# Layer 0 of a hybrid decoder trunk: a written-out TensorE order for the S5 quarters, the projections, the gates and the linear unit

## The chip, the cores and the metric

The kernel runs on one core of a Trainium2 chip. The metric is the device time of one execution in microseconds (us). The engines are named as the profile names them: PE (TensorE, matrix products; PEld its weight loads), DVE (VectorE), ACT (ScalarE), POOL (GpSimd) and SP (SyncE, which here issues every DMA).

## The reference

The reference takes `x` of 1024 tokens by 1024 features through two residual layers, all in float32. The change touches layer 0 alone:

```python
def even_layer(hn, ...):
    q, k, v, gate_a, u, gate_b = split_cols(hn @ w_in, EVEN_SPLITS)   # 512, 128, 128, 512, 512, 512
    q = rms_norm(q.reshape(bsz, L, 8, 64), q_g)
    k = rms_norm(k.reshape(bsz, L, 2, 64), k_g)
    att = swa_sink_attention(q, k, v, sinks, rel_bias) * jax.nn.silu(gate_a)
    ssm = s5_mixer(u, ...) * jax.nn.silu(gate_b)
    return jnp.concatenate([att, ssm], axis=-1) @ w_out
```

`swa_sink_attention` is banded: each block of 128 queries sees its own and the previous block of keys, with a bias by distance and a sink in the softmax. `s5_mixer` is a complex diagonal state space (32 groups of 16 channels, 64 states), then `gelu`, then the gated linear unit `h = y @ glu_w + glu_b`, `h[:, :512] * sigmoid(h[:, 512:])`. Layer 1 (an indexer that picks the top 256 keys, attention over them, gate, output projection) stays as it is.

## The kernel before, in words

Activations lie transposed, features on the partitions. Each float32 product is made of three fp32r products: both factors are split into a high part and the rest, and hi x hi, hi x lo, lo x hi are summed in PSUM. Weights come as a stream of chunks of 256 output columns (`wstream`; `load_w`, L135): one DMA of 1 MB, a copy to `whi` on ACT (L153) and a subtraction to `wlo` on POOL or DVE (L154). Chunks listed in `LO_ON_V` (L126) are split in four pieces with DVE; the others in one piece of 128x2048 with POOL.

Layer 0 has these stages in the order of the program text:

- The first chunk of `u` is projected while `x` arrives (L317 to L341); the squares give the RMS factors `rr` and, by a round trip through DRAM, `rb` (L342 to L349).
- S5 parameters on DVE (L393 to L516), from scalars to the powers of the decay.
- `u_chunk(0)`, then keys and values (L541 to L556): eight token tiles of 24 products of 256 columns, per-head norms in `norm_heads` (L351: squares on ACT with a sum each, `rstd_of` L197 and a product with `rr` on POOL at L199, L200 and L360, scaled copies on ACT at L362), a transposition by PE.
- The distance table `gt` (32 copies, L563 to L567, on DVE).
- Four S5 quarters (`s5_quarter`, L578). Each builds `Q` (DVE, L602 to L607), `W` (POOL, L609 to L616) and the rotations `Tb` (DVE, L623 to L628), transposes `Q` (L635), makes a small kernel matrix `M` (L640 to L654, with eight DMAs), multiplies the states' input (L663, 32 products), scans on DVE (L667 to L687: products with `Tb`, eight scans, the result `X`), and gets the output by L694 (with `M`) and L696 (with `X`), with a gelu on ACT (L698). `u_chunk(1)` stands after the first quarter.
- `q_chunk(0)` and `q_chunk(1)` (L367): 16 tiles of 24 products of 256 columns with the same norms, two transpositions each (L375), then out to DRAM.
- The banded attention: 16 units (8 blocks by 2 key heads). `swa_scores` (L743) makes eight score products, adds the bias and takes the maximum on DVE (L756), exponentials on ACT (L761) and the division on DVE or POOL. `swa_out` (L771) runs `SWA_AHEAD` = 4 units later: transpositions (L777), copies, products with `v` (L783).
- `gate_chunk` four times (L382): 16 groups of 48 products of 256 columns, a product with `rb` on DVE (L389), out to DRAM unactivated.
- The linear unit (L810 to L868): `y` is split into `y_hi` and `y_lo` (L822, L823), eight groups of 24 products of 512 columns (L855 to L857), Sigmoid of the linear unit's gate (L861) and of the branch's gate (L863), three products and the split into `cat` (L864 to L868). Then the attention's result is read back, gated by Sigmoid (L875), two products, and split into `cat` (L876 to L879).
- The output projection and the residual (L886 to L919), then layer 1.

Only SP's queue has a written order at the very start (L310). On all other engines a list scheduler orders the instructions of layer 0 at build time, by the program's order as priority and by its own estimate of durations; each engine then runs its list strictly in order. So PE runs the gates, which stand after the attention in the text, among the S5 quarters and the attention. Layer 1 has two stretches with a written PE order (`manual_schedule`, L1083 and L1555); there a `Filler` (L1385) draws pieces of other work between the steps of the main work.

## Time and profile before

| what | value |
|---|---|
| median of three runs | 1107.06 us (1104.15 to 1111.34) |
| profiled execution, its own time | 1109.46 us |
| its span on the core | 1107.7 us |
| mean granted PE clock | 0.971 |
| PE, DVE, ACT, POOL busy | 93%, 72%, 54%, 43% of the span |

Between the profiled execution's time and its span lie 1.8 us. Times in rows count from the start of the span. Busy is the time in which at least one instruction of the engine runs; "idle before" is the gap ahead of an instruction, with what ended it. Matrix products overlap, so the distance from the start of one to the start of the next is what one costs in a row of them. PEclk is the mean share of full clock granted in a stretch; the granted level is either 1.0 (2.4 GHz) or 0.5 (1.2 GHz). The stretch in which the change lies runs from 43 us (end of the first `u` chunk) to 418 us (first product of the output projection).

### The profile page before, as it was taken

The numbers are of one execution on the slowest core, as the hardware profiler recorded it, in microseconds if no ns is written. First come the engines' busy times: TensorE is split into PE (matmuls) and PEld (weight loads), VectorE is DVE, ScalarE is ACT, GpSimd is POOL, SyncE is SP. The second block draws the span as 40 slices with busy tenths as digits, with TensorE's granted clock in tenths as the row PEclk, the third lists the DMA queues.
The fourth block names the chain that finished last, engine by engine and source line by source line (L and its number), as shares of the span: only waits on it lengthen the run. The fifth ranks groups of instructions, "written<-read, shape, count | busy, mean of one in ns | idle before, by whom it ended". The sixth has DMA issues, their size and how long they took to land.

```text
span 1107.7 us, 19105 instructions
## 1 busy us (share of the span) xinstructions
PE 1026.0 (93%) x6533; PEld 900.1 (81%) x6533; DVE 797.0 (72%) x1768; ACT 598.6 (54%) x1563; POOL 475.7 (43%) x667
## 2 busy tenths in 40 slices
PE   6799888999999789999799999999998889999998
PEld 4687877898776567887689999999886768998898
DVE  6899987717553795367668759889877989778742
ACT  7343554215543642344356699969954777565620
POOL 3356876232121283224322367867522554445000
PEclk9899998999999889999899999999999999999999
DMA  7228542683321623545002103022326686665323
GB/s 257 96 78 272 147 123 65 173 235 127 95 77 39 247 80 110 199 166 164 4 1 96 63 29 102 39 87 78 115 77 201 213 263 176 190 196 163 113 91 119
DMA packets 105585, 143.05 MB, mean 129 GB/s; under 512 B 9568, under 2 KB 80104, under 8 KB 100624
## 3 DMA queue, kind: packets, MB, share of 16 engines
q1 hardware_dynamic: 105488, 141.84, 40.9%
q8 instruction: 51, 0.84, 0.3%
q14 instruction: 46, 0.38, 0.1%
HBM read 104.93 MB, written 38.31 MB: 129 GB/s over the span
## 4 chain that ended last, share of the span: by engine, by line
PE 60%; DVE 19%; DMA 7%; ACT 5%; issue 4%; POOL 4%; SPq 1%; DVEq 0%; ACTq 0%; POOLq 0%
PE mm L230 7%; PE mm L231 7%; PE mm L232 7%; PE mm L217 4%; PE mm L216 4%; PE mm L218 4%; PE psx L783 2%; PE mm L1497 2%; PE mm L1498 2%; PE mm L1496 2%; PE tr L1365 2%; DMA xt<-in_xT_dram 1%; DVE xh L917 1%; PE tr L777 1%; PE mm L1380 1%
## 5 line engine op out<-in xcount | busy, mean ns | idle before, releaser
L154 POOL TENSOR_TENSOR wlo<-wraw,whi 128x512 fp32r<-128x512 f32 (+1 forms) x43 | 95.0, 2233 | 120.5 <-ACT whi L153 107.6
L153 ACT CAST whi<-wraw 128x512 fp32r<-128x512 f32 (+2 forms) x117 | 83.5, 770 | 79.6 <-PE mm L231 29.2
L1338 POOL TENSOR_TENSOR bt<-bt,mk 128x384 f32<-128x384 f32 (+3 forms) x80 | 85.4, 1084 | 77.7 <-DMA bt<-g_d 70.2
L216 PE MATMUL mm<-whi,h1T_hi 128*128 128x256 f32 x384 | 110.5, 289 | 0.0
L218 PE MATMUL mm<-whi,h1T_lo 128*128 128x256 f32 x384 | 110.0, 288 | 0.0
L217 PE MATMUL mm<-wlo,h1T_hi 128*128 128x256 f32 x384 | 109.9, 287 | 0.0
L1199 DVE TENSOR_SCALAR_CACHE_REDUCE vjunk<-sc,vt 128x512 bf16<-128x512 uint16 (+5 forms) x90 | 91.1, 1012 | 3.0
L230 PE MATMUL mm<-hT_hi,whi 128*128 128x256 f32 (+1 forms) x288 | 87.5, 304 | 0.6 <-DVE uT L533 0.6
L231 PE MATMUL mm<-hT_lo,whi 128*128 128x256 f32 (+1 forms) x288 | 87.1, 302 | 0.0
L232 PE MATMUL mm<-hT_hi,wlo 128*128 128x256 f32 (+1 forms) x288 | 86.9, 302 | 0.0
L1233 ACT ACTIVATE sjunk<-sc,st 128x384 bf16<-128x384 uint16 (+5 forms) x90 | 77.2, 858 | 6.4 <-POOL st L1237 4.1
L154 DVE TENSOR_TENSOR wlo<-wraw,whi 128x512 fp32r<-128x512 f32 (+1 forms) x74 | 57.6, 815 | 24.9 <-ACT whi L153 20.6
L1496 PE MATMUL mm<-aT_hi,whi 128*128 128x256 f32 x256 | 73.5, 287 | 1.2 <-ACT aT_hi L1470 1.2
L1497 PE MATMUL mm<-aT_lo,whi 128*128 128x256 f32 x256 | 73.1, 285 | 1.0 <-DVE aT_lo L1471 1.0
L216 PEld LDWEIGHTS mm<-whi,h1T_hi 128*128 128x128 f32 x384 | 73.1, 191 | 0.6
L217 PEld LDWEIGHTS mm<-wlo,h1T_hi 128*128 128x128 f32 x384 | 73.2, 191 | 0.3
L218 PEld LDWEIGHTS mm<-whi,h1T_lo 128*128 128x128 f32 x384 | 73.1, 191 | 0.3
L1498 PE MATMUL mm<-aT_hi,wlo 128*128 128x256 f32 x256 | 73.2, 286 | 0.0
L362 ACT ACTIVATE st<-mm,nr 128x64 f32<-128x64 f32 (+1 forms) x160 | 45.4, 356 | 51.0 <-POOL nr L360 47.0
L1056 DVE SCALAR_TENSOR_TENSOR sc<-relu,wi,sc 128x384 f32<-128x384 f32 (+3 forms) x70 | 49.4, 707 | 20.5 <-ACT relu L1051 16.6
L1349 ACT ACTIVATE s<-s,mn 128x128 f32<-128x128 f32 (+7 forms) x64 | 49.5, 774 | 26.6 <-DVE mn L1343 26.5
L216 PE MATMUL mm<-whi,hT_hi 128*128 128x256 f32 x192 | 58.0, 303 | 4.4 <-ACT st L362 2.7
(386 smaller groups left out, 3515.9 us busy)
## 6 DMA issues: line engine op xcount, KB each, us to landing
wraw<-in_w_dram SPq DMA_DIRECT2D x20, 1024.0 KB, 5.2
wraw<-in_wo_dram SPq DMA_DIRECT2D x16, 1024.0 KB, 5.4
bt<-g_d SPq DMA_DIRECT2D x24, 256.0 KB, 3.7
g_d<-g1r_d SPq DMA_DIRECT2D x8, 576.0 KB, 9.1
bt<-g_d SPq DMA_DIRECT2D x24, 192.0 KB, 3.2
qT_d<-gst SPq DMA_DIRECT2D x32, 128.0 KB, 2.1
qT<-qT_d SPq DMA_DIRECT2D x32, 128.0 KB, 3.1
xh<-in_xT_dram SPq DMA_DIRECT2D x16, 256.0 KB, 3.2
```

Source lines behind the costliest of these rows:

```text
L154: eng.tensor_sub(lo[p_], raw[p_], rd(hi[p_]))
L216: T.matmul(ps, a, hi[:, k, c0:c1], start=(k == 0), stop=False)
L217: T.matmul(ps, a, lo[:, k, c0:c1], start=False, stop=False)
L218: T.matmul(ps, b, hi[:, k, c0:c1], start=False, stop=(k == 7))
L230: T.matmul(o, a, hT[0][:, k, ts], start=(k == 0), stop=False)
L231: T.matmul(o, a, hT[1][:, k, ts], start=False, stop=False)
L232: T.matmul(o, b, hT[0][:, k, ts], start=False, stop=(k == 7))
L1199: V.tensor_scalar(junk[:, :128 * (b + 1)], data(b), self.thr(j), None, op0=OP.is_ge, op1=OP.add, accum_out=self.cnt[:, it, j:j + 1])
L1338: G.tensor_add(bt, bt, mk[b][:, ks])
L1496: T.matmul(ps, a, aT[0][:, k, toks], start=(k == 0), stop=False)
L1497: T.matmul(ps, a, aT[1][:, k, toks], start=False, stop=False)
L1498: T.matmul(ps, b, aT[0][:, k, toks], start=False, stop=(k == 7))
```

## The change

The list of what it does:

- From the keys and values on to the end of the linear unit, PE's order is the order of the text (`manual_schedule` for PE). All other engines keep the list scheduler.
- Projections, gates and the linear unit become one generator of pieces (`fill`): keys and values, `u_chunk(1)`, the two `q` chunks, the four gate chunks, the linear unit. A piece carries an estimate in us. `fill(us)` draws pieces for so much estimated time. Transpositions behind the norms are drawn `LAG` = 7.0 estimated us after the products of their tile.
- `s5_quarter` is cut at six places. `fill` is called ahead of the quarters (36), after each of four parts of a quarter (4, 4, 16, 6) and once ahead of the attention (12); `Q` and `Tb` of the next quarter are emitted two parts ahead.
- The attention is cut finer: a unit's four score pairs alternate with transpositions of an earlier unit and with products with `v` of the one before that; `fill(1.1)` stands twice in each unit until four of the eight groups of the linear unit are done. The other four groups follow the attention.
- A gate group has 24 products of 512 columns in place of 48 of 256; at its eviction the silu is made by `x * (1 + tanh(x/2))` (twice the silu) with one ACT and one more DVE operation; halves and quarters are put right later. The gate of the attention is applied as the attention leaves PSUM, that of the S5 branch in the linear unit's eviction, whose result goes to DRAM (`go_d`) and comes back for the split into `cat`.
- `rstd_of` and the product with `rr` are emitted at high priority for keys and queries; `gt` is filled by ACT; every weight chunk is split in four pieces; `s` has 4 buffers in place of 6, `nms` 4 in place of 2.

```diff
+LAG = 7.0
+S5_FILL = (36.0, 4.0, 4.0, 16.0, 6.0, 12.0)
+SWA_FILL = 1.1
...
-        return (hi, lo), [piece, WSTEP if i in LO_ON_V or i == 21 else 8, 0]
+        return (hi, lo), [piece, WSTEP, 0]
...
-        r = rstd_of(stg, ms[:, :nh], nh, "nr")
-        if t is not None:
-            G.tensor_tensor(r, r, bc(rr[:, 0, t:t + 1], [128, nh]), op=OP.mult)
+        with tc.high_priority() if t is not None else ExitStack():
+            r = rstd_of(stg, ms[:, :nh], nh, "nr")
+            if t is not None:
+                G.tensor_tensor(r, r, bc(rr[:, 0, t:t + 1], [128, nh]), op=OP.mult)
...
+    def lagged(n, products, rest):
+        for i in range(n):
+            out = products(i)
+            later.append([LAG, lambda i=i, out=out: rest(i, out)])
+            yield 2.8
...
+    def gate0_pieces(dst, f0):
+        w = wstream.get()
+        for f in range(2):
+            for half in range(2):
+                ps = ps_mm.tile([128, 512], F32, name="mm")
+                for k in range(8):
+                    a, b_ = (x[:, k, f * 128:f * 128 + 128] for x in w)
+                    h_, l_ = (x[:, k, half * 512:half * 512 + 512] for x in hT)
+                    T.matmul(ps, a, h_, start=(k == 0), stop=False)
+                    T.matmul(ps, a, l_, start=False, stop=False)
+                    T.matmul(ps, b_, h_, start=False, stop=(k == 7))
+                    if k % 2 and k < 7:
+                        yield 1.4
                 st = stg.tile([128, 512], F32, name="gst", bufs=2)
                 V.tensor_mul(st, ps, rb[:, half * 512:(half + 1) * 512])
+                S.activation(ps, st, AF.Tanh, scale=0.5)
+                V.scalar_tensor_tensor(st, ps, 1.0, st, op0=OP.add, op1=OP.mult)
                 dma(dst[f0 + f, :, half * 512:(half + 1) * 512], st)
+                yield 1.4
...
+    class Filler:
+        def __call__(self, us):
+            self.owed += us
+            while self.owed > 0:
+                got = next(self.gen, None)
+                if got is None:
+                    break
+                self.owed -= got
+                for x in later:
+                    x[0] -= got
+                while later and later[0][0] <= 0:
+                    later.pop(0)[1]()
...
+    def glu_pieces():
+        es_h0.close()
...
+                S.copy(yh, yv)
+                V.tensor_sub(yl, yv, rd(yh))
+        yield 0.0
...
+                    S.activation(sg, pp[0], AF.Tanh, scale=0.5, bias=glub[:, 1, 4 + n:5 + n])
+                    V.scalar_tensor_tensor(sg, sg, 1.0, gt_, op0=OP.add, op1=OP.mult)
+                    V.scalar_tensor_tensor(sg, pp[1], glub[:, 0, n:n + 1], sg, op0=OP.add, op1=OP.mult)
+                    dma(go_d[n, :, t0:t0 + 512], sg)
+                    glu_done.append(n)
+                    yield 1.4
...
+    fill = Filler(chain(kv_pieces(), u_pieces(1), q_pieces(0), q_pieces(1), gate0_pieces(ga_d, 0), gate0_pieces(ga_d, 2),
+                        gate0_pieces(gb_d, 0), gate0_pieces(gb_d, 2), glu_pieces()))
+    es_pe.enter_context(tc.manual_schedule(engines={mybir.EngineType.PE}))
+    fill(S5_FILL[0])
...
-            GE.tensor_copy(gt[:, z0:z1], bc(rbt[:, r:r + 1], [8, z1 - z0]))
+        S.copy(gt[:, z0:z1], bc(rbt[:, r:r + 1], [8, z1 - z0]))
...
+    for qi in range(4):
+        cur, nxt = nxt, s5_quarter(qi + 1) if qi < 3 else iter((0, 0))
+        for part, ahead in enumerate((False, True, False, True)):
+            if ahead:
+                next(nxt)
+            next(cur)
+            fill(S5_FILL[1 + part])
...
-            at = sw.tile([128, 4, 128], F32, name="at", bufs=1)
-            S.copy(at, po)
+            at = gates.pop(0)
+            V.scalar_tensor_tensor(at, po, 0.5, at, op0=OP.mult, op1=OP.mult)
...
+        if done:
+            out = swa_out(*done.pop(0))
+        if u >= SWA_AHEAD - 1 and flight:
+            tr = swa_tr(*flight.pop(0))
+        for part in range(4):
+            next(sco, None)
+            next(out if part > 1 else tr, None)
+            if part % 2 and len(glu_done) < 4:
+                fill(SWA_FILL)
...
+    to_cat(0, range(6))
+    while len(glu_done) < 6:
+        next(fill.gen)
+    to_cat(0, range(6, 8))
+    for _ in fill.gen:
+        pass
+    to_cat(1, range(8))
```

A `yield` in `s5_quarter` stands after the DMAs of `Wp` (behind `Q` and `W`), after `Tb`, after the copy `kr`, after the DMAs of `M`, after `X` and after the output.

## Rows read from the trace of the kernel before

**Rows 1.** Page, part 1: busy time of each engine over the whole span

```profile
PE 1026.0 (93%) x6533; PEld 900.1 (81%) x6533; DVE 797.0 (72%) x1768; ACT 598.6 (54%) x1563; POOL 475.7 (43%) x667
```

**Rows 2.** Busy time by stretch, with granted clock, DMA share and GB/s

```profile
core 0: us, PE busy (x) PEld busy (x) DVE busy (x) ACT busy (x) POOL busy (x), PEclk, DMA share, GB/s
43.00:240.00 197.00, 175.12 (x1325) 163.09 (x1323) 155.49 (x408) 80.79 (x311) 115.53 (x169) 0.95 0.52 150
240.00:363.00 123.00, 120.43 (x823) 95.81 (x821) 62.93 (x250) 49.89 (x170) 25.89 (x12) 1.00 0.31 96
363.00:418.00 55.00, 42.54 (x157) 33.02 (x158) 47.74 (x40) 31.58 (x45) 31.45 (x16) 0.88 0.47 169
418.00:480.00 62.00, 62.00 (x271) 50.41 (x271) 26.96 (x35) 19.83 (x33) 15.26 (x9) 1.00 0.53 177
...
848.00:1040.00 192.00, 176.11 (x1079) 152.90 (x1079) 160.52 (x417) 128.54 (x263) 90.20 (x90) 0.97 0.64 194
```

**Rows 3.** Who PE waited for, 43 to 418: us in total, times, longest

```profile
PE tr L375 <- ACT st L362: 9.1, 5, 4.4
PE mm L855 <- ACT sg L861: 6.3, 1, 6.3
PE mm L855 <- DVE sg L866: 4.8, 2, 3.9
```

**Rows 4.** PE's groups by line, 43 to 418: count, busy, mean ns, idle before

```profile
L230 PE MATMUL mm<-hT_hi,whi 128*128 128x256 f32 x256 | 74.4, 290 | 0.0
```

**Rows 5.** Timeline of PE: start, duration; 256-column and then 512-column products in a row

```profile
64.24 0.28 PE L216 MATMUL mm<-whi,hT_hi 128*128 128x256 f32 x1
64.36 0.28 PE L217 MATMUL mm<-wlo,hT_hi 128*128 128x256 f32 x1
...
73.47 0.40 PE L230 MATMUL mm<-hT_hi,whi 128*128 128x512 f32 x1
73.70 0.39 PE L231 MATMUL mm<-hT_lo,whi 128*128 128x512 f32 x1
```

**Rows 6.** Timelines of POOL and ACT: the norm of one query tile, with the wait

```profile
139.68 0.23 POOL L199 TENSOR_SCALAR nr<-nms 128x4 f32<-128x4 f32 x1
...
141.25 1.14 POOL L200 TENSOR_TENSOR nr<-nr,neghalf 128x4 f32<-128x4 f32 x1
...
143.64 0.72 POOL L360 TENSOR_TENSOR nr<-nr,rr 128x4 f32<-128x4 f32 x1
...
144.39 0.93 ACT L362 ACTIVATE st<-mm,nr 128x64 f32<-128x64 f32 x4 [4.20 <-POOL nr L360]
```

**Rows 7.** Timelines of PE and DVE: third S5 quarter, input product to output product

```profile
164.71 1.97 PE L663 MATMUL ps<-U,QT 128*64 128x128 f32 x32
...
170.44 0.69 DVE L667 TENSOR_TENSOR tmp<-ps,Tb 128x512 f32<-128x512 f32 x1
...
183.76 1.41 DVE L687 TENSOR_TENSOR X<-tmp 64x512 f32<-64x512 f32 x2
...
187.49 0.38 PE L696 MATMUL ps<-X,Wp 128*128 128x128 f32 x2
```

**Rows 8.** Timeline of ACT: exponentials of one attention unit

```profile
294.00 0.51 ACT L761 ACTIVATE s<-s,nm 128x256 f32<-128x256 f32 x1 [0.94 <-DVE nm L757]
...
294.51 0.49 ACT L761 ACTIVATE s<-s,nm 128x256 f32<-128x256 f32 x1
```

**Rows 9.** ACT's groups by line, 43 to 418: count, busy, mean ns, idle before

```profile
L822 ACT CAST y_hi<-yr 128x512 fp32r<-128x512 f32 x8 | 8.2, 1115 | 0.0
...
L698 ACT ACT_TABLE_LOAD x1 | 1.3, 1283 | 0.0
L761 ACT ACT_TABLE_LOAD x1 | 1.3, 1283 | 0.0
L863 ACT ACT_TABLE_LOAD x1 | 1.3, 1283 | 0.0
```

**Rows 10.** ACT's groups by line, 600 to 900: table loads in layer 1

```profile
L1349 ACT ACT_TABLE_LOAD x1 | 1.3, 1283 | 0.0
```

More of the change, by code (lines that the diff above doesn't have):

```diff
@@ L259, in tile_hybrid_swa_s5_dsa @@
     att_d = dr.tile([4, 128, L], F32, name="att_d")
+    go_d = dr.tile([4, 128, L], F32, name="go_d")
     y_d = dr.tile([4, 8, 16, 8, 128], F32, name="y_d")
@@ L380, in q_chunk @@
                 dma(qT_d[n, 2 * c:2 * c + 2, :, i * 128:(i + 1) * 128].rearrange("j p t -> p j t"), rd(qt[:, n]))
-    def gate_chunk(dst, f0):
+        yield from lagged(NT, products, rest)
+    def gate0_pieces(dst, f0):
         w = wstream.get()
@@ L401, in tile_hybrid_swa_s5_dsa @@
     dsk = s5.tile([128, 512], F32, name="dsk")
+    es_b = ExitStack()
+    bp = es_b.enter_context(tc.tile_pool(name="bias0", bufs=1, side="right", reuse_waits="tile"))
+    rbt = bp.tile([8, 32], F32, name="rbt")
+    dma(rbt, rbias)
+    gt = bp.tile([8, FZ], F32, name="gt")
+    for r in range(32):
+        hi_d = BUCKET_LO[r + 1] if r < 31 else 1024
+        z0 = 1024 - hi_d
+        z1 = 1024 - BUCKET_LO[r] if r else FZ
+        S.copy(gt[:, z0:z1], bc(rbt[:, r:r + 1], [8, z1 - z0]))
+    dma(g1r_d, gt)
     with tc.tile_pool(name="s5p", bufs=1, side="right", reuse_waits="tile") as sp:
@@ L559, in tile_hybrid_swa_s5_dsa @@
-    with tc.tile_pool(name="bias0", bufs=1, side="right", reuse_waits="tile") as bp:
-        rbt = bp.tile([8, 32], F32, name="rbt")
-        dma(rbt, rbias)
-        gt = bp.tile([8, FZ], F32, name="gt")
-        for r in range(32):
-            hi_d = BUCKET_LO[r + 1] if r < 31 else 1024
-            z0 = 1024 - hi_d
-            z1 = 1024 - BUCKET_LO[r] if r else FZ
-            GE.tensor_copy(gt[:, z0:z1], bc(rbt[:, r:r + 1], [8, z1 - z0]))
-        dma(g1r_d, gt)
+    es_b.close()
     s5q = es_s5.enter_context(tc.tile_pool(name="s5q", bufs=1, side="right", reuse_waits="tile"))
@@ L768, in swa_scores, with swa_tr @@
                 V.tensor_scalar(s[:, g, :w], s[:, g, :w], den[:, g:g + 1], None, op0=OP.mult)
-        return s
-    def swa_out(b, kv, s, po):
-        w = 256 if b else 128
-        nk = w // 128
+        flight.append((b, kv, s))
+        yield
+    def swa_tr(b, kv, s):
+        nk = 2 if b else 1
+        pTs = []
+        done.append((b, kv, pTs))
         for kk in range(nk):
@@ L782, in swa_out @@
                 S.copy(pT, pt)
+            pTs.append(pT)
+            yield
+    def swa_out(b, kv, pTs):
+        if kv == 0:
+            pos[0] = ps_x.tile([128, 4, 128], F32, name="psx")
+        po, nk = pos[0], len(pTs)
+        for kk, pT in enumerate(pTs):
             T.matmul(po[kv * 64:(kv + 1) * 64], vt[:, b - nk + 1 + kk, kv * 64:(kv + 1) * 64], pT,
                      start=(kk == 0), stop=(kk == nk - 1), tile_position=(0, kv * 64))
+            if kk + 1 < nk:
+                yield
         if kv:
-            at = sw.tile([128, 4, 128], F32, name="at", bufs=1)
-            S.copy(at, po)
+            at = gates.pop(0)
+            V.scalar_tensor_tensor(at, po, 0.5, at, op0=OP.mult, op1=OP.mult)
             dma(att_d.rearrange("g p t -> p g t")[:, :, b * 128:(b + 1) * 128], at)
-    flight = []
+    fill(S5_FILL[5])
+    flight, done, gates, pos = [], [], [], [None]
     for u in range(16 + SWA_AHEAD):
+        sco = tr = out = iter(())
         if u < 16:
@@ L869, in tile_hybrid_swa_s5_dsa, with to_cat @@
-    for half in range(2):
-        for g in range(4):
-            at = st3.tile([128, 512], F32, name="at", bufs=4)
-            dma(at, att_d[g, :, half * 512:(half + 1) * 512])
-            ga = gat[:, g, half * 512:(half + 1) * 512]
-            sb = st3.tile([128, 512], F32, name="sb")
-            S.activation(sb, ga, AF.Sigmoid)
-            V.tensor_mul(at, at, ga)
-            G.tensor_mul(at, at, sb)
-            S.copy(cat[half][0][:, g], at)
-            V.tensor_sub(cat[half][1][:, g], at, rd(cat[half][0][:, g]))
+    def to_cat(half, gs):
+        if len(cat) <= half:
+            cat.append(tuple(cps[1 - half].tile([128, 8, 512], F32R, name=f"cat_{n}") for n in ("hi", "lo")))
+        ca = cat[half]
+        for g in gs:
+            at = st3.tile([128, 512], F32, name="at", bufs=6)
+            dma(at, (att_d if g < 4 else go_d)[g % 4, :, half * 512:(half + 1) * 512])
+            if g < 4:
+                S.copy(ca[0][:, g], at)
+                V.tensor_sub(ca[1][:, g], at, rd(ca[0][:, g]))
+            else:
+                S.activation(ca[0][:, g], at, AF.Copy, scale=0.25)
+                V.scalar_tensor_tensor(ca[1][:, g], at, 0.25, rd(ca[0][:, g]), op0=OP.mult, op1=OP.subtract)
```

224 lines of the change are left out of this document (102 added, 122 removed).

## The prediction

> **What bounds the kernel now.** The page's busy times come first: PE is busy for 93% of the span and DVE for 72% [rows 1], so PE sets the time wherever it is fed. The second view is the busy time by stretch. The change lies between 43 and 418 us, 375 us long. PE is busy there for 175.1 + 120.4 + 42.5 = 338.1 us, so it is idle for 36.9 us [rows 2]. The clock tells of a second loss: a mean of 0.95 over 197 us means that the half level was granted for 2 x 0.05 x 197 = 19.7 us, and 0.88 over 55 us means 13.2 us; what PE did there would have taken half the time at full clock, so up to 16.4 us are lost [rows 2]. Together 53.3 us of the stretch are no work at full clock. The output projection behind it is busy for 62.0 of 62.0 us at clock 1.00 [rows 2]: whatever ends the linear unit earlier moves all that follows by as much.
>
> The third view, who PE waited for, tells what the 36.9 us are. The longest are transpositions behind the norms of queries (L375 on the scaled copies of L362: 9.1 us in 5 waits) and two holes in the linear unit, 6.3 and 4.8 us, in which PE waits for evictions of its PSUM tiles [rows 3]. The holes come where PE's list has nothing else at hand: in the linear unit the gates are used up.
>
> **The change part by part.** The products are the same but for their width, so the sum is: what is lost now, plus the saving on width, less what the new order loses.
>
> *Width.* 16 gate groups have 48 products of 256 columns each, 768 in all (L230 has 256 of them, L231 and L232 as many) [rows 4]. A 256-column product costs 0.12 us from start to start, a 512-column one 0.23 us [rows 5]. 384 wide ones in place of two narrow ones each save 384 x 0.01 = 3.8 us; starts are read to 0.01 us, so the bounds are 0 and 8, and I take 3.
>
> *The linear unit beside the attention.* From 363 to 418 us PE is idle for 12.5 us and loses 6.6 us to the clock [rows 2], 19 us that the new place of the work could win. In the attention PE runs 823 products, of which 60 + 120 + 128 = 308 are the attention's own and 515 are gates; at 0.12 us the gates take 62 us and the attention's own work 58 us, 3.7 us for each of 16 units. The written order gives each unit 2 x 1.1 = 2.2 us of pieces: a unit of 5.9 us where it took 123 / 16 = 7.7 us. Does the softmax keep up? A unit's exponentials cost 4 x 0.51 = 2.0 us on ACT [rows 8]; with the maxima before and the division behind I estimate 6 us from last score to transposition, and the order leaves two units, 11.8 us. So it does, with two exceptions. The split of `y` can start only when the last gate product has released `hT`'s space, and PE reaches the linear unit one `fill` later; the eight copies at 1.1 us on ACT [rows 9] also stand ahead of exponentials. Bounds 0 and 9 us (all eight in the open); I take 4, nearest to the first copies and their subtractions. And when pieces have run out (33.6 estimated us of them before four groups of the linear unit are done, some 15 units), the last units wait for their own softmax: two units without scores last some 2 x (3.7 - 8 x 0.12) = 5.5 us, about as long as the softmax, and the copies behind the transpositions are no longer covered either; bounds 0 and 8, I take 4. The other four groups, 11 us for each pair, cover the return of `go_d`, so I count nothing for the split into `cat`; without that cover its last round trip would show, some 6 us.
>
> *The quarters in parts.* Between L663 and the products with `X` the order draws 16 us of pieces. In the third quarter DVE took from 170.44 to 185.17, 14.7 us, for that chain, and PE reached L696 22.8 us after L663 began [rows 7], because DVE was held by something else first. DVE's other work of a quarter (`Q` and `Tb` of the next one) now stands ahead of the chain or behind it. A quarter lasts some 40 us on PE (30 of pieces, 10 of its own), and DVE's busy share was 155.5 of 197 us [rows 2], so DVE should be free in time from the second quarter on; in the first, the parameters push it late. Per quarter the wait is between 0 and 22.8 - 16.4 = 6.4 us; I take 3 for the first and 1 for each other, 6 in all, range 0 to 26.
>
> *Norms.* A query tile waited 4.2 us between its squares and its copies, and the three POOL operations, 2.1 us of work, ran from 139.68 to 144.36 because other POOL work stood between them [rows 6]. High priority puts them together, so the wait should be 2 to 4.2 us; with squares and copies (0.93 us) the tile is ready 4 to 6.5 us after its products. `LAG` leaves two tiles of products, 2 x 24 x 0.12 = 5.7 us. So 0 to 0.8 us for each of 16 tiles; I take 3 us, with bounds 0 and 13.
>
> *Start and rest.* PE's transposition of `rr` stands ahead of the written order, and keys no longer fill the time before it: 4 us, bounds 0 and 6 (what PE loses there now is inside the 36.9). For PSUM tiles not released in time, the start of the attention and DMAs I take 4, bounds 0 and 9. The 32 copies of `gt` go from DVE to ACT, which is busy for 81 of 197 us [rows 2]: nothing. Splitting POOL's share of the weights into four pieces adds instructions to an engine busy for 116 of 197 us: nothing on PE's path, and shorter waits for the norms. If POOL were full, both would show up in the norms' term.
>
> *Clock.* New idle time is 4 + 4 + 6 + 3 + 4 + 4 = 25 us. Now 36.9 us of idle time go with 16.4 us of clock; by that ratio it would be 11. The new waits are shorter than the holes of 4 to 6 us that go [rows 3], so I take 4, range 0 to 16.
>
> *Sum.* 53.3 + 3 - 25 - 4 = 27 us gained. The profiled execution goes from 1109.46 to 1082.4; it stood 2.4 us above the median of 1107.06, from which the same gain gives 1080 us. With all low ends the gain is 56 and the time 1051; with all high ends (6 + 9 + 8 + 26 + 13 + 9 + 16 = 87) it is 31 us slower, 1138. All ends at once are unlikely.
>
> *A rule against the change.* The table of gelu is loaded once for all four quarters (L698), that of the exponential once (L761), that of Sigmoid once (L863), each 1.28 us [rows 9]; layer 1 loads the exponential's anew after its tanh gates [rows 10]. Now tanh runs among the gelus and among the exponentials. If each change of function loaded a table, two more loads for each of the last two quarters would be hidden on ACT; in the attention, some six evictions would each bring two loads into a softmax chain. The Trainium skill (ScalarE: Activation LUTs, "Table sets: the hidden batching unit") says that every switch to another set costs a load, and that exponential and tanh share one set; by that rule nothing is loaded in the attention, and two of the loads of before go. No row of before shows the two functions under one table.
>
> **The rivals.**
>
> *Few waits.* The order fits, and less than 12 us are lost: 56 less 8 to 12 gives a gain of 44 to 48, near 1061. For it: PE is idle for 2.6 of 123 us in the attention of before, where it always has pieces at hand [rows 2]. Against it: the S5 chain of 14.7 us is barely covered [rows 7].
>
> *The waits only move.* Layer 1's written order from 848 to 1040 has PE idle for 15.9 of 192 us and loses up to 5.8 us to the clock, 11.3% [rows 2]; the stretch of before loses 53.3 of 375, 14.2%. At 14 to 16% on some 319 us of work 52 to 61 us are lost, and the gain is between 4 and -5: 1107. For it: a list in fixed order can't step round a late operation, as the scheduler could at build time. Against it: that stretch of layer 1 has little to draw from.
>
> *Slower: the scan chain decides.* Place: DVE's queue at L667 of each quarter. If `Q` of the next quarter (some 7 us of DVE work as I read it from the second quarter) stands in the queue when L663 is done, the chain ends 6.4 + 7 = 13.4 us late, four times 13.4 = 54, and each wait is long enough for the clock to fall: 7 us more. In place of the 6 and 4 us above that loses 29 - 10 + 61 = 80: 24 us slower, 1131. It decides from 8 us for each quarter on, where the gain is used up. For it: DVE is busy for 79% of that stretch [rows 2]. Against it: 40 us of PE work for each quarter stand beside at most 155.5 / 4 = 39 of DVE, parameters and evictions of before included.
>
> *Tables in the attention.* Twelve loads of 1.28 us make 15 us on ACT, of which I let 8 show: 1088.
>
> **How the numbers follow.** Forecast 0.56 (1066 to 1095), few waits 0.16, tables 0.04, the waits only move 0.14, scan chain 0.10. The likeliest gives 1080 us; the range 1058 to 1107 leaves out the best of the few-waits case and the slower cases. Around 1% (11 us) is about what a measurement of this kernel can tell from no change: faster 0.76, same 0.14, slower 0.10.
>
> **What would show it.** In the profile after, 43 us to the first product of the output projection should last some 348 us, with PE idle for about 25 and its clock at 0.98 or more; the linear unit's holes should be gone from the list of waits. L696 waiting for `X` by more than 5 us in a quarter speaks for the scan chain; table loads between exponentials for that rival; waits of transpositions on L362 beyond 10 us would put the norms' term wrong. The forecast is wrong if the stretch lasts over 364 or under 333 us.

## The result, and the profile after

The changed kernel takes 1142.95 us (median of 4 runs, 1137.70 to 1144.02) where the kernel before takes 1107.60 beside it: 1.031 times as long, 95% interval 1.026 to 1.036. It is slower by 35 us by the medians (34 by the ratio) where 27 us were to be gained, and lies beyond the forecast's range.

One reading of the text ahead must be put right first. The first product of the output projection in the kernel before starts at 426.24 us, not at 418: from 417.76 on PE runs the last 36 products of the linear unit without a hole. So the stretch in which the change lies was 383.2 us long, and the forecast of 348 for it is 356 by the right boundary; no term of the sum hangs on this. These are the two starts, in PE's timelines of before and of after:

```profile
426.24 0.39 PE L230 MATMUL mm<-cat_hi,whi 128*128 128x512 f32 x1
```

```profile
463.45 0.39 PE L233 MATMUL mm<-cat_hi,whi 128*128 128x512 f32 x1
```

The stretch from 43 us became 420.5 us long, 37.2 more. Behind it 3.2 us are regained (the span grew by 34.0), so the loss lies in the stretch. Busy time by stretch of the changed kernel: up to 112 us comes the first quarter's `Q`, 305 is the first score product, 423 the last.

```profile
core 0: us, PE busy (x) PEld busy (x) DVE busy (x) ACT busy (x) POOL busy (x), PEclk, DMA share, GB/s
43.00:112.00 69.00, 41.73 (x243) 36.03 (x243) 48.04 (x202) 20.50 (x73) 31.15 (x65) 0.84 0.46 142
112.00:305.00 193.00, 177.85 (x1125) 154.83 (x1124) 117.70 (x224) 70.53 (x269) 90.22 (x127) 0.95 0.40 119
305.00:423.00 118.00, 98.54 (x409) 64.71 (x410) 75.08 (x256) 55.69 (x172) 25.94 (x17) 0.90 0.40 111
423.00:463.00 40.00, 37.07 (x139) 24.18 (x139) 15.12 (x27) 11.26 (x24) 1.89 (x1) 0.86 0.48 151
```

PE is busy for 355.2 of the 420 us to 463, so it is idle for 64.8 us where [rows 2] had 36.9, and the mean clock is below 0.95 in three of four stretches. The half level was granted most where PE had stood longest (0.84 in the first row). The list of PE's waits from 43 to 463 us, the counterpart of [rows 3]:

```profile
engine line waited for: us in total, times, longest us
PE ps L756 <- DVE Q L717: 17.5, 1, 17.5
PE psx L881 <- DVE mx L883: 16.2, 21, 4.6
PE tr L416 <- ACT st L367: 12.8, 4, 8.2
PE tr L395 <- POOL st L369: 4.2, 2, 2.2
PE mm L219 <- ACT st L367: 3.4, 1, 3.4
PE tr L908 <- POOL s L894: 2.9, 1, 2.9
PE mm L522 <- DVE y_lo L505: 2.2, 2, 1.9
PE mm L219 <- DVE uT L461: 2.2, 1, 2.2
PE ps L820 <- DVE X L810: 1.6, 1, 1.6
```

Three waits carry the loss. The first is one hole, at 92.6 us, in which PE waits for `Q` of the first quarter. The second are 21 short stops of the attention's score products (4.6 us the longest), each for a PSUM tile `psx` that DVE has not read yet. The third are transpositions behind the norms.

Which tile the score products wait for can be read from PE's and DVE's timelines side by side. Two heads share one `psx` tile, and the text writes the two products of the second head (L881, L882) right behind those of the first or behind four transpositions. PE's timeline, first and second head of one tile, then DVE's:

```profile
313.97 0.22 PE L881 MATMUL psx<-kT,qT 128*128 128x128 f32 x1
314.03 0.28 PE L882 MATMUL psx<-kT,qT 128*128 128x128 f32 x1
314.70 0.33 PE L881 MATMUL psx<-kT,qT 128*128 128x128 f32 x1 [0.39 <-DVE mx L883]
```

```profile
314.34 0.29 DVE L883 CUSTOM_DVE_ANT_0 s<-psx,bm 128x128 f32<-128x128 f32 x1 [0.92 <-PE psx L882]
314.56 0.08 DVE L883 DVE_READ_ACCUMULATOR2_ANT mx<- 128x1 f32 x1
```

The second head starts 0.06 us after DVE's reduction of the first. So it is for all 21 stops: each falls on the second head of a tile, none on a first head, which takes a fresh tile. PE does not wait for another tile to come free, but for the reduction of the head that it has just written to the same tile.

The linear unit's holes of before are gone, as foreseen, and the scan (L820 for `X`) costs 1.6 us in all.

The hole of 17.5 us leads to SP's queue. Its timeline from 34 to 59 us:

```profile
34.47 0.30 SPq L568 DMA_DIRECT2D g1r_d<-gt  x1
37.45 4.55 SPq L830 DMA_DIRECT2D g_d<-g1r_d  x7
...
42.79 0.59 SPq L830 DMA_DIRECT2D g_d<-g1r_d  x1
44.90 0.30 SPq L351 DMA_DIRECT2D r_d<-rt  x1
58.21 0.35 SPq L352 DMA_DIRECT2D rb<-r_d  x1
58.61 0.41 SPq L578 DMA_DIRECT2D aa<-in_sa_dram  x1
```

And in DVE's timeline, the first wait behind it:

```profile
61.92 3.28 DVE L461 TENSOR_TENSOR uT<-ps,rb 128x512 f32<-128x512 f32 x3 [18.03 <-DMA rb<-r_d]
```

The same issues in the kernel before, from SP's timeline:

```profile
13.32 2.50 SPq L410 DMA_DIRECT2D aa<-in_sa_dram  x1
...
49.67 0.33 SPq L347 DMA_DIRECT2D r_d<-rt  x1
51.29 0.33 SPq L348 DMA_DIRECT2D rb<-r_d  x1
...
85.47 5.65 SPq L704 DMA_DIRECT2D g_d<-g1r_d  x8
```

In the changed kernel `gt` is ready at 34 us, so its replication, eight DMAs of 576 KB each, goes out just ahead of `r_d`, a store of 4 KB. The load `rb`, which needs that store landed, goes out 13.3 us later; in the kernel before it is 1.6 us, where the replication starts at 85 us only. And the S5 parameters' load `aa` goes out at 58.61 us where it went out at 13.32 before. DVE, in order, stands still for 18 us, and all of its S5 work comes late.

### The profile page after: what moved, and what is told of

It reads as the page before. It is cut to its first block, busy times and chain, and to the rows that moved or that the text cites. A ratio compares the mean times of both kernels' runs of the same rounds, so it can differ in the third digit from the quotient of the medians.

```text
span 1141.7 us, 18421 instructions
## 1 busy us (share of the span) xinstructions
PE 1034.4 (91%) x6149; PEld 879.5 (77%) x6149; DVE 780.9 (68%) x1753; ACT 599.5 (53%) x1618; POOL 454.2 (40%) x684
## 4 chain that ended last, share of the span: by engine, by line
PE 45%; DVE 7%; DMA 3%; ACT 3%; issue 2%; POOL 2%; SPq 0%; DVEq 0%; ACTq 0%; POOLq 0%
PE mm L233 5%; PE mm L234 5%; PE mm L235 5%; PE mm L219 3%; PE mm L220 3%; PE mm L221 3%; PE mm L1594 2%; PE mm L1595 2%; PE mm L1593 2%; PE tr L1474 2%; DVE xh L1026 1%; DMA bt<-g_d 1%; POOL wlo L157 1%; PE mm L1489 1%; DVE s L1452 1%
## 5 line engine op out<-in xcount | busy, mean ns | idle before, releaser
L157 POOL TENSOR_TENSOR wlo<-wraw,whi 128x512 fp32r<-128x512 f32 x76 | 105.7, 1421 | 145.4 <-ACT whi L156 145.4
L156 ACT CAST whi<-wraw 128x512 fp32r<-128x512 f32 (+1 forms) x150 | 86.5, 643 | 77.7 <-DMA wraw<-in_wo_dram 29.6
L219 PE MATMUL mm<-whi,h1T_hi 128*128 128x256 f32 x384 | 109.5, 287 | 0.0
L219 PEld LDWEIGHTS mm<-whi,h1T_hi 128*128 128x128 f32 x384 | 72.7, 190 | 0.6
L367 ACT ACTIVATE st<-mm,nr 128x64 f32<-128x64 f32 (+1 forms) x160 | 45.2, 357 | 36.7 <-POOL nr L365 32.3
L1165 DVE SCALAR_TENSOR_TENSOR sc<-relu,wi,sc 128x384 f32<-128x384 f32 (+3 forms) x70 | 49.5, 708 | 20.1 <-ACT relu L1160 16.2
L219 PE MATMUL mm<-whi,hT_hi 128*128 128x256 f32 x192 | 58.0, 302 | 5.5 <-ACT st L367 3.4
L1477 ACT CAST pT_hi<-tr 128x512 fp32r<-128x512 f32 x72 | 41.4, 578 | 39.1 <-PE tr L1474 35.7
L233 PE MATMUL mm<-h1T_hi,whi 128*128 128x512 f32 (+1 forms) x160 | 59.8, 374 | 0.0
L234 PE MATMUL mm<-h1T_lo,whi 128*128 128x512 f32 (+1 forms) x160 | 59.7, 373 | 0.0
```

Of the source, the lines that this page charges most:

```text
L156: S.copy(hi[p_], raw[p_])
L157: eng.tensor_sub(lo[p_], raw[p_], rd(hi[p_]))
L219: T.matmul(ps, a, hi[:, k, c0:c1], start=(k == 0), stop=False)
L233: T.matmul(o, a, hT[0][:, k, ts], start=(k == 0), stop=False)
L234: T.matmul(o, a, hT[1][:, k, ts], start=False, stop=False)
```

## The experiments

Theories: the early table (B), the written order of PE (O), the attention's own chain (P). The first four kernels take one part each; where a later expectation uses P or another letter, it says what for. Ratios are to the kernel before, measured beside each; the changed kernel is at 1.031.

**Is it the order or what it orders?** The written order is taken out of layer 0; everything else of the change stays.

```diff
-    es_pe.enter_context(tc.manual_schedule(engines={mybir.EngineType.PE}))
```

> The changed kernel without any written order of PE in layer 0: the same instructions, ordered by the scheduler. If the written order is what costs (theory O), this comes to 1107 or below. If the early bias table costs the 18 us hole whatever the order (theory B), the hole is partly filled with projections that the scheduler takes forward, and the time is 1115 to 1130. If neither order nor table decides but the attention's new content (gate at the division, linear unit beside it), 1135 to 1145.

Measured: 1097.27 us, ratio 0.991 (0.987 to 0.994). The first product of the output projection comes at 417.65 us, 45.8 earlier. Theory O holds: what the change orders is worth 10 us, and the written order loses more than all of it. The early table is in this kernel too: PE waits 3.1 us for `Q`, not 17.5, though `Q` is no earlier (the first product with `CB` is at 116.6 us, in the change at 112.0). In the scheduler's order other work stands there.

**The attention alone left to the scheduler.**

```diff
     fill(S5_FILL[5])
+    es_pe.close()
     flight, done, gates, pos = [], [], [], [None]
```

> The changed kernel, with PE's written order ended ahead of the attention: from there on the scheduler orders PE as it did in the kernel before. Theory O (the written order loses the 20 to 30 us that PE idles or runs at half clock in 304 to 463 us): 1115 to 1125, and the waits of the score products for psx go. Theory P (the unit is bound by the chain score, maximum on DVE, exponentials, division, transposition and by three PSUM tiles, whatever the order): 1138 to 1148.

Measured: 1113.08 us, ratio 1.005 (1.002 to 1.008). That is 2 us below the range of theory O and far from that of P. Theory O holds for the attention: the score products' waits for DVE's reductions shrink to 0.5 us, and 30 us come back.

**`gt` back on DVE, behind the S5 parameters.**

```diff
-        S.copy(gt[:, z0:z1], bc(rbt[:, r:r + 1], [8, z1 - z0]))
...
     es_b.close()
+    with tc.tile_pool(name="bias0", bufs=1, side="right", reuse_waits="tile") as bp:
...
+            GE.tensor_copy(gt[:, z0:z1], bc(rbt[:, r:r + 1], [8, z1 - z0]))
```

> The changed kernel with one part undone: the 32 copies of gt are on DVE again, behind the S5 parameters. Theory B (the early bias table is at fault: gt is done at 34 us, its replication of 4.7 MB goes on the queues ahead of rb, which makes DVE wait 18 us, and PE then waits 17.5 us for the first quarter at 92.6 us): the wait at L756 shrinks below 3 us, the first product of the output projection comes near 440 us and the time near 1120 (1113 to 1126). Rival W (the written order is at fault, the hole stays because PE has nothing else in its list there): the hole keeps over 10 us and the time stays at 1135 or more.

Measured: 1126.9 us, ratio 1.017 (1.012 to 1.021). The wait for `Q` is gone and the output projection starts at 448.26 us, 15.2 earlier. The time lies 1 us above the range of theory B and the start 8 us behind the 440 that it named, but far from rival W: undoing the early table is worth 16 us. Which part of it costs, the transfers, the copies or the room, this run doesn't tell.

**The early table alone, in the kernel before.**

> The kernel before with one part of the change alone: gt made by ACT ahead of the S5 parameters. Theory B: rb lands some 10 us later than its 54.95 us and the S5 parameters with it; the time is 1112 to 1125. If the replication delays only what has slack, or the scheduler fills the gap with projections and gates, the time stays within 1104 to 1110, and then the table costs only together with the written order.

Measured: 1107.99 us, ratio 0.999 (0.997 to 1.001). The table delays the parameters here as well (`aa` at 58.5 us, first product with `CB` at 116 us where it was 95), and PE waits 6.8 us for `Q`; the total does not change, because the scheduler filled the time with projections and gates. The table costs only together with a fixed order.

**What about the table?** First its transfers are held behind `rb`:

```diff
+    with tc.issue_after(rb_in.ins):
+        dma(g1r_d, gt)
-    dma(g1r_d, gt)
```

> The changed kernel; gt stays early on ACT, but its store g1r_d, and with it the eight replications, is issued behind the load of rb. If the transfers ahead of rb are what costs (theory B), this is as good as gt back on DVE: 1123 to 1130, with the wait at L756 below 4 us. If the copies on ACT are what costs (they stand ahead of ACT's other work), it stays at 1138 to 1145.

Measured: 1132.55 us, ratio 1.022 (1.020 to 1.024): 10 of the 16 us. `rb` goes out 2.0 us behind `r_d`, but `aa` still at 47 us, and PE waits 8.5 us for `Q`. Neither of the two expectations had this. In the kernel with the table back, `aa` goes out at 14.9 us. What is different is the room: the change opens the pool of `gt` below that of the parameters. So the room was taken early, with the copies back on DVE and in their old place in the text; the cut is against the kernel with the table back.

```diff
+    es_b = ExitStack()
+    bp = es_b.enter_context(tc.tile_pool(name="bias0", bufs=1, side="right", reuse_waits="tile"))
...
+    gt = bp.tile([8, FZ], F32, name="gt")
...
     with tc.tile_pool(name="s5p", bufs=1, side="right", reuse_waits="tile") as sp:
```

> As gt back on DVE, but the pool of rbt and gt is opened ahead of that of the S5 parameters, as in the change; copies and store stay late, on DVE. If the room alone makes the parameters late, aa is loaded near 47 us (15 us with the pool late, 58 us in the change), DVE's parameters start near 54, PE waits 5 to 10 us for Q, and the time is 1130 to 1136 where 1127 was without and 1133 with the table's transfers held back. If the room has no part in it, aa is loaded at 15 us and the time is 1124 to 1129.

Measured: 1137.99 us, ratio 1.027 (1.023 to 1.031). The expectation of a late table failed in its own way. With the parameters pushed back DVE had nothing to do at 26 us, and the scheduler made the copies there; the transfers went out at 38 us again. PE's waits in this kernel, then SP's queue:

```profile
PE ps L756 <- DVE Q L717: 15.3, 1, 15.3
```

```profile
46.01 0.30 SPq L351 DMA_DIRECT2D r_d<-rt  x1
...
58.62 1.09 SPq L572 DMA_DIRECT2D aa<-in_sa_dram  x1
```

With gt's copies on DVE the hole is 15.3 us, nearly the change's 17.5. So the engine that makes the copies has no part in it that these times show (1.027 and 1.031, with overlapping intervals). The pool opened early is enough to bring 11 of the 16 us: the parameters' loads come 32 us and more later, and the table comes early. It is not the room alone, for here too the replication stands ahead of `rb`; with the transfers held back, room and copies left 6 us. Which tile held the parameters' room until then was not followed.

**The two losses together.** Table back and the attention left to the scheduler:

> The changed kernel with gt back on DVE and PE's written order ended ahead of the attention. If the two losses add up, 16 for the table and 30 for the attention, it is at 1097 (1093 to 1101), and the written order among the quarters costs nothing by itself. If the order among the quarters costs too (theory O for the whole layer), it stays at 1103 or more, and only the kernel without any written order reaches 1097.

Measured: 1098.37 us, ratio 0.992 (0.990 to 0.995). They add up. Among the quarters the written order, as it stands, comes out as good as the scheduler's (0.992 and 0.991), if the early table costs the scheduler's order nothing here, as it cost nothing in the kernel before. What the attention loses is seen best between this kernel and the one with the table back alone; here are their stretches from the first score product to the output projection, first with the written attention, then without:

```profile
290.00:448.00 158.00, 135.83 (x549) 89.02 (x548) 90.11 (x284) 68.29 (x198) 27.74 (x18) 0.89 0.41 122
```

```profile
289.00:417.00 128.00, 115.33 (x543) 79.91 (x541) 82.03 (x276) 65.17 (x193) 31.26 (x21) 0.97 0.48 139
```

The same products take 158 and 128 us. Idle time is 22.2 against 12.7 us; by the mean clock the half level lost up to 0.11 x 158 = 17.4 against 0.03 x 128 = 3.8 us. The two make up to 23 of the 30 us; the other 7 were not split.

**More filler in a unit.** If the unit's length were given by its chain, what is written between would be free.

```diff
-SWA_FILL = 1.1
+SWA_FILL = 2.0
...
-            if part % 2 and len(glu_done) < 4:
+            if part % 2 and len(glu_done) < 8:
```

> gt back on DVE, and the written order kept, with more of the linear unit in each unit of the attention: 2.0 for 1.1 us of pieces at two places, up to all eight groups for four. Theory F (a unit lasts 7.2 us whatever is written into it, by its chain, so what fills it is free): the attention keeps its 117 us, the 41 us from its last score to the output projection fall to about 20, and the time to 1107 (1103 to 1112) from 1127. Theory P (PE's list stalls at the score products whatever lies between, so each piece lengthens its unit): the attention gets longer by what the tail gets shorter, 1122 to 1130.

Measured: 1125.93 us, ratio 1.016 (1.013 to 1.019), no different from 1.017. The scores now take 134.5 us (from 117.5), and what follows them 19.7 (from 40.3). Theory F falls: each piece made its unit longer, and the stops at `psx` stayed (12.5 us).

**The same filler behind each part.**

```diff
-            if part % 2 and len(glu_done) < 8:
+            if len(glu_done) < 8:
```

(with `SWA_FILL` 1.0.)

> As the kernel with more of the linear unit in each unit of the attention (4.0 us of pieces a unit, all eight groups), but written behind each of the four parts (1.0 us each) and not behind every second. Theory S (a score product waits for its PSUM tile because the last but one stands too close ahead of it in the list for DVE's reduction of 0.42 us and what DVE has queued): the waits for psx fall from 12.5 us to below 5, and the time from 1126 to about 1118 (1114 to 1121). If the waits come from DVE's queue whatever the distance, or from the units' chain, they stay above 10 us and the time within 1122 to 1130.

Measured: 1115.06 us, ratio 1.007 (1.005 to 1.010): 10 us gained with the same pieces, so their spacing matters. The waits for `psx` fell to 8.6 us in 11 stops, not below 5, so theory S is met in the time and missed in the waits. The trace says what the spacing does: 1.0 us of pieces now stands between the two heads of a tile, and DVE reduces the first meanwhile. Why the second head has to wait for the reading of the first, in another part of the tile, no run shows. The 11 stops that are left, like the 18 of the kernel with pieces behind every second part, all fall on the second head of a tile. They end when DVE's reduction does, which can be late by what DVE has queued. A tile for each head, or another number of tiles, was not run, and the cut of `s` from 6 buffers to 4 was not undone by itself.

**The norms.** First a longer lag, one size changed (`LAG` 7.0 to 10.0):

> gt back on DVE, and one size changed: transpositions follow their norms at a lag of 10 for 7 us of pieces, one product more. Transpositions wait for scaled copies (L416) 18 us in two waits in the kernel with gt back. If the lag is simply too short by some microseconds, both waits shrink by 2.8 us: 1119 to 1123. If GpSimd's queue (weight pieces ahead of the norms' square roots) makes the norm late by whatever it holds, the waits move to the next query and the time stays at 1124 to 1129.

Measured: 1120.05 us, ratio 1.011 (1.009 to 1.013). The time came as the first theory had it, but most of the waits did not go, they changed places: transpositions no longer wait, and projections (L219) wait 16.4 us in 4 stops for their evictions, where they waited 3.4 in one. What makes the norms late can be read in GpSimd's queue. From its timeline, the kernel with the table back, while PE waits 10.6 us for the first query's copies:

```profile
106.94 2.77 POOL L157 TENSOR_TENSOR wlo<-wraw,whi 128x512 fp32r<-128x512 f32 x2
109.67 0.44 POOL L711 TENSOR_TENSOR W<-tmpg 128x64 f32<-128x64 f32 x1
...
110.47 2.72 POOL L157 TENSOR_TENSOR wlo<-wraw,whi 128x512 fp32r<-128x512 f32 x2
113.16 0.72 POOL L708 TENSOR_TENSOR tmpg<-W,pw 128x256 f32<-128x256 f32 x1
...
114.65 0.55 POOL L202 TENSOR_SCALAR nr<-nms 128x4 f32<-128x4 f32 x1
```

ACT has the squares ready at 106.8; the norm's first step on GpSimd (L202) starts at 114.65, behind four weight pieces of some 1.4 us and the powers of `W`. So the pieces went to DVE, which makes one in some 0.8 us (page, part 5):

```diff
-    LO_ON_V = (0, 2) + tuple(range(13, 21)) + tuple(range(29, 39))
+    LO_ON_V = tuple(range(21)) + tuple(range(29, 39))
```

> gt back on DVE, and the low halves of all of layer 0's weights made by DVE where GpSimd made eleven of thirteen chunks. Theory G (the queries' norms are late because their square roots stand behind weight pieces and powers of W in GpSimd's queue): the two waits of transpositions on L367, 18 us, fall below 8, and the time from 1127 to about 1116 (1111 to 1121). If the powers of W alone hold the norms, the waits stay above 14 us and the time within 1123 to 1130; if DVE becomes the late one, the waits move to Q or uT and the time stays as well.

Measured: 1102.59 us, ratio 0.997 (0.994 to 1.000), 24 us against the table back alone and 8 below the range of theory G. The waits of transpositions on L367 fall from 18.2 to 8.3 us, 9.9 of the 24; the first score product comes 17.3 us earlier. The rest is gained behind it, not by fewer stops (`psx` 20.0 us, from 16.5) but at a clock of 0.93 from the first score product to the output projection, where it was 0.89. So theory G holds for the norms, and a good part of the gain isn't theirs. Its stretch of quarters has the clock at 0.98, where the kernel with the table back had 0.94:

```profile
91.00:273.00 182.00, 172.81 (x1106) 151.31 (x1105) 122.19 (x249) 69.60 (x267) 61.87 (x107) 0.98 0.47 140
```

Undoing the change's cut of GpSimd's pieces (four of two rows where it was one of eight), with the table back:

```diff
-        return (hi, lo), [piece, WSTEP, 0]
+        return (hi, lo), [piece, WSTEP if i in LO_ON_V or i == 21 else 8, 0]
```

> gt back on DVE, and one more part of the change undone: GpSimd makes each weight chunk's low half in one piece of eight rows again, where the change cuts it into four of two. If the cutting made the norms late (it lets the pieces in between the steps of the norm), transpositions wait less than the 18 us on L367 and the time falls from 1127 to 1115 to 1121. If one long piece (some 5.5 us) holds the norms as long as four short ones, it stays within 1123 to 1131.

Measured: 1123.38 us, ratio 1.011 (1.007 to 1.014), not to be told apart from 1.017 (1.012 to 1.021); the waits on L367 are 21.1 us, no less. The cut did not make the norms late. And the pieces on DVE in the kernel before:

> The kernel before, with the low halves of layer 0's weights made by DVE. If GpSimd's queue is as much in the way of its norms (9.1 us of waits on L362), 1097 to 1102. If the scheduler's own order has something else for PE in those waits, or DVE is the fuller engine there (137 of 157 us busy from 43 to 200), 1104 to 1115.

Measured: 1100.85 us, ratio 0.991 (0.989 to 0.994). It helps the old order too, but not by the reason given: the waits on L362 are 13.5 us there, more than the 9.1 of [rows 3], while the linear unit ends 10.6 us earlier (output projection at 415.65). So a relieved GpSimd is worth something in either order; that it works through the queries' norms is seen only in the written one.

**All mends together**, first with the attention left to the scheduler:

> What the runs so far name, together: gt back on DVE, the written order ended ahead of the attention, the weights' low halves on DVE, a lag of 10 us for the transpositions. The first two give 1098; if the norms' waits (17 us of PE in the written quarters) are what is left there, the other two bring 8 to 14 us: 1084 to 1090, faster than both kernels. If these waits only trade places with others, 1094 to 1100.

Measured: 1084.46 us, ratio 0.980 (0.977 to 0.984), faster than both kernels and the best of the study. The time is the one expected, but the waits have only in part gone: no transposition waits on L367, projections wait for it 13.2 us in 4 stops (3.4 without the last two mends), and 4.3 us go to `Q`. PE's idle time from 43 us to the first score product falls from 27.4 to 17.2 us, and its clock rises from 0.94 to 0.96. Then with the written order kept to its end:

> The written order kept through the attention, with four mends: gt back on DVE, weights' low halves on DVE, lag 10, and 1.0 us of the linear unit behind each of the four parts of a unit, up to all eight groups. If the three named hindrances are all that the order loses by, the gains add up: 1127 less 24 (pieces) and 12 (fill) is 1091, with the lag 1086 to 1093, within 8 us of the kernel with the attention left to the scheduler (1084.5). If a written order costs by itself, 1097 or more.

Measured: 1103.59 us beside a kernel before of 1111.28, ratio 0.994 (0.991 to 0.996). The gains don't add up: the order of the attention still costs 1.3%, 15 us, against the kernel above. Up to the first score product the two are alike (275.4 and 275.0 us). Then, in three stretches, the written one first:

```profile
275.00:310.00 35.00, 24.38 (x96) 18.91 (x97) 22.25 (x65) 20.04 (x45) 3.66 (x3) 0.82 0.58 176
310.00:394.00 84.00, 83.41 (x378) 57.22 (x377) 49.56 (x180) 35.08 (x115) 9.73 (x5) 0.99 0.34 104
394.00:424.00 30.00, 19.05 (x79) 9.31 (x78) 14.96 (x46) 10.10 (x34) 3.78 (x2) 0.89 0.36 112
```

```profile
275.00:310.00 35.00, 32.06 (x141) 24.51 (x140) 26.28 (x85) 23.62 (x57) 5.16 (x4) 0.90 0.70 191
310.00:377.00 67.00, 65.91 (x309) 46.44 (x309) 44.41 (x137) 26.97 (x84) 6.09 (x4) 0.99 0.39 125
377.00:407.00 30.00, 22.84 (x98) 10.97 (x94) 17.10 (x69) 14.56 (x52) 5.68 (x3) 0.96 0.32 100
```

With enough filler, spread, the middle is full: PE is busy for 83.4 of 84 us. The order loses at both ends: 10.6 us idle in the first 35 us (2.9 in the free one) and 11.0 in the last 30 (7.2), each with the clock down. At the start the `y` split's copies stand in ACT's and DVE's queues; PE waits there 7.1 us for `psx`, again on second heads alone, and 2.0 for `y_hi`. At the end nothing is left to fill with.

Last, no written order at all, with table back and pieces on DVE:

> No written order in layer 0, gt back on DVE, the weights' low halves on DVE: the same instructions as in the kernel with the attention alone left free (1084.5, lag apart). If the written order of the quarters gains by itself what the forecast gave it, this is slower, 1090 to 1098; if it only costs nothing, 1081 to 1088; if the scheduler is better there too, below 1080.

Measured: 1087.68 us, ratio 0.985 (0.982 to 0.989). Its interval and that of the best kernel (0.977 to 0.984) overlap, and the two differ in the lag as well; whether the written quarters gain anything stays open.

## Why the prediction was wrong

The sign of the content was right: the same instructions in the scheduler's order gain 10 us. Four terms of the sum failed: three prices of the fixed order, and the clock that went with them.

*"The 32 copies of `gt` go from DVE to ACT ...: nothing."* This was the step that failed by kind. It asked whether ACT has time, and it has. It did not follow the move to the DMAs that the copies release, nor to the room that the S5 parameters now get later. Measured: 15 to 16 us, 10 of them given back by holding the transfers behind `rb`. The scheduler's order hides all of it (0.999), so the step was also one of a cover that the change itself takes away.

*"Does the softmax keep up? ... So it does."* It looked at the far end of the chain, from score to transposition, and that end kept up: transpositions wait 2.9 us. What failed was the near end, which the estimate of the unit left out: the products of a tile's second head wait for DVE's reduction of the first, and DVE comes to it in its own order. Only the last term, "For PSUM tiles not released in time, the start of the attention and DMAs I take 4, bounds 0 and 9", had a price for it; these stops alone are 16.2 us. Scores lasted 117 us, 7.3 us a unit, not 5.9. With the split and the drain, priced at 4 each, the stretch from the first score to the output projection takes 157.7 us where the scheduler needs 128.4. The kernel with four mends shows that the ends keep costing when the middle is mended.

*"So 0 to 0.8 us for each of 16 tiles; I take 3 us."* Priority orders the scheduler's list; it does not make a queue empty. The norm steps still stood among weight pieces and powers of `W`: 12.8 us of waits in the change, beyond the 10 that the prediction itself had set as the sign against this term, and 18.2 with the table back, where the bound was 13. The sentence "If POOL were full, both would show up in the norms' term" named the right place and gave it no price.

*Clock, 4 us.* With the idle time at 64.8 and not 25 us, the clock went with it: by the mean clocks of the first four rows above up to 0.16 x 69 + 0.05 x 193 + 0.10 x 118 + 0.14 x 40 = 38 us, where the stretch lost up to 16.4 before.

So the gap of some 64 us at the output projection (+37 for -27) can be laid out roughly by three runs: 15 for the table; 14 for the weight pieces on GpSimd (17.3 up to the first score product, less the 3 priced for the norms), of which the norms' waits themselves are 9.9; 29 for the attention, less the 12 priced for its split, its drain and its PSUM tiles. That makes 46. The other 18 were not split by a run, and the clock is in all of these figures.

What held: the holes of the linear unit are gone; the scan waits 1.6 us where 6 were taken; a wide product starts 0.23 us ahead of what follows it (386.76 and 386.99 in the last list below). No table is loaded between exponentials and tanh. ACT's loads from 43 to 470 us, which answer to [rows 9]:

```profile
L599 ACT ACT_TABLE_LOAD x1 | 1.3, 1283 | 0.0
L822 ACT ACT_TABLE_LOAD x1 | 1.3, 1283 | 0.0
L890 ACT ACT_TABLE_LOAD x1 | 1.3, 1283 | 0.0
```

One load (L890, at 308.08 us) serves all 64 exponentials and the tanh evictions (L529) among them. The Trainium skill (ScalarE: Activation LUTs, "Table sets: the hidden batching unit") says that the two share a set; the trace agrees. The two loads that the prediction saw go by that rule are gone: that of Sigmoid, and the reload in layer 1 [rows 10], where ACT has no load at all now. The load for gelu (L822, at 149.88 us) also serves tanh: the gates' tanh (L440) runs from 211.6 us on, among gelus that go on to 288.2, with no load until 308.08.

Of the rivals, the scan chain gave the nearest number, 1131, at the wrong place. "The waits only move" gave the right mechanism, a fixed list that can't step round a late operation, and priced it at 1107: it took its rate of loss, 14 to 16%, from layer 1's written order, and this one loses up to 64.8 + 38 of 420 us, 24%. The edits in the scheduler's order (0.999 for the table) show that step round at work.

## What to carry to other kernels

A written order takes away the cover under which other edits were free. Price each of them again as if every late operation showed, and follow an early producer to its transfers and to the room that it holds. Before PE's order is fixed, look in the in-order queues of its suppliers, and ask of each product not only when its operands are there but when its PSUM tile has been read. Where two products share a PSUM tile, write something between them that lasts as long as the first one's reduction. And an order may be closed ahead of the part that it hurts: with nothing else changed, closing it ahead of the attention took the kernel from 1142.95 to 1113.08 us, and with the table back from 1126.9 to 1098.37. With the other mends it stands at 0.980 of the kernel before, where the order kept to its end stands at 0.994. That a written order gained anything here, against the scheduler's order of the same instructions, no run shows.

## What the runs showed of the hardware

A 4 KB store behind 4.7 MB of replication took 13.3 us until its reader could be issued, against 1.6 us in the kernel before (`r_d` to `rb`). The Trainium skill (DMA: Bandwidth & Descriptors, "HWDGE ordering" in "Queues, rings and completion order") says that each DMA engine takes up the descriptors of a ring in their order, but that nothing holds a later one back until an earlier one has finished. The trace agrees with the first half: the small store, issued last, was late by what SP had issued ahead of it, and with the replication issued behind `rb` it took 2.0 us.

The two score products of a pair start 0.12 us apart behind products of the linear unit, and 0.22 us apart behind a transposition or a product with `v`. PE's timeline of the changed kernel:

```profile
386.76 0.39 PE L523 MATMUL mm<-y_hi,wlo 128*128 128x512 f32 x1
386.99 0.28 PE L881 MATMUL psx<-kT,qT 128*128 128x256 f32 x1
387.11 0.28 PE L882 MATMUL psx<-kT,qT 128*128 128x256 f32 x1
387.23 0.60 PE L908 MATMUL tr<-ident,s 128*128 128x128 f32 x4
388.03 0.38 PE L881 MATMUL psx<-kT,qT 128*128 128x256 f32 x1 [0.20 <-DVE mx L883]
388.25 0.28 PE L882 MATMUL psx<-kT,qT 128*128 128x256 f32 x1
```

All 30 pairs of the attention that follow a transposition or a product with `v` are of the slow kind, 16 of them without a stop ahead, and 22 of the 25 that follow a wide product of the fast one; the other three stand in stretches where wide products start 0.43 us apart, at the half level of the clock. 30 x 0.1 = 3 us. Why is not known.
